# A modulation group moved beside the last two attention heads, and one exponential per block of queries

## The chip, the cores and the metric

The kernel runs on one core of a Trainium2 chip. The metric is device time in microseconds (us) of one execution. The core has five engines: TensorE (PE, matrix products; its weight loads are listed apart as PEld), VectorE (DVE), ScalarE (ACT), GpSimd (POOL) and SyncE (SP), which issues most of the transfers. Each engine works through its own queue in order and waits at an instruction until its data and buffers are there. TensorE writes its results to PSUM, eight banks of 128 partitions x 512 fp32; everything else lies in SBUF.

## The reference

One inference step of a backbone with two layers, width 1024, on 1154 positions: 128 context tokens, a gap of 2, and 1024 latent tokens on a grid 64 wide. In each layer a mixer and a feed-forward part read a normalised input that is scaled and shifted by modulation vectors, and are added back through a gate. The change lies in the modulation and the attention of layer 0:

```python
mc = jnp.split(sc @ w_mod[i] + b_mod[i], N_MOD, axis=-1)    # context: 6 vectors of 1024
ml = jnp.split(sl @ w_mod[i] + b_mod[i], N_MOD, axis=-1)    # latent tokens
hl = rmsnorm(xl, norm_mix[i]) * (1 + ml[1]) + ml[0]         # needed first
q, k, v, p = even_project(hl, w_in_ab[j], q_gain[j], k_gain[j])
# per row of the grid and head; kb, vb: an 8-row neighbourhood; ck, cv: 256 cached context keys
s_loc = jnp.einsum("bqhd,bkhd->bhqk", qi, kb) * scale + bi[None]
s_ctx = jnp.einsum("bqhd,bkhd->bhqk", qi, ck) * scale
pr = jax.nn.softmax(jnp.concatenate([s_loc, s_ctx], axis=-1), axis=-1)
out = pr[..., :n_local] @ vb + pr[..., n_local:] @ cv
...
xl = xl + ml[2] * yl                                        # needed after the out projection
hl = rmsnorm(xl, norm_ffn[i]) * (1 + ml[4]) + ml[3]
xl = xl + ml[5] * conv_ffn(hl, ...)
```

So the six modulation vectors of a layer are six slices of one product of two rows (`sc`, `sl`) with a 1024 x 6144 matrix. The kernel computes them as three *groups* of 2048 columns: group 0 holds vectors 0 and 1, group 1 holds 2 and 3, group 2 holds 4 and 5. Only group 0 is needed before the projections; groups 1 and 2 are first used after the attention. Softmax is taken over 384 local positions (with some masked by the bias) and 256 context keys together.

## The kernel before

**Numbers.** Values are f32. For TensorE each operand is split into a high part and a rest (`whi` and `wlo` of a weight, `hhi` and `hlo` of the input), and a product is three matmuls. A weight block of 128 x 1024 is loaded into `wraw` (L237), copied to `whi` on ScalarE (L253), and the rest `wlo` is made on GpSimd (L255). `wraw`, `whi` and `wlo` have two buffers each in the pool `wp`.

**Order.** Python generators emit the work, and a scheduler then orders the instructions of each engine by data, priorities and buffers.

**A modulation group** (`mod_group`) has 16 *steps*, eight blocks of 128 input channels by two halves of the columns. A step loads 512 KB of `wmod` (L301, tile `mraw`) and issues two f32 matmuls of 512 columns each (L304, `sc` holds the two rows, padded to 32; the profile has four records for a step); their sum stands in the tile `modps`, in one PSUM bank for the group's whole time. The two matmuls of a step and those of its neighbour write different quarters of that bank's partitions (`g = 64 * u + 32 * x`). At the end `mod_spread` turns the result into columns (tiles `modev`, `modt`) with a few small matmuls.

**Layer 0's mixer**, in the order of time:

1. Norm and group 0 (to some 66 us).
2. `project_v`: the values of nine blocks of tokens in two passes, six and three blocks (PSUM `vps`, six banks of the pool `psm`). Each pass reads the four `wv` blocks.
3. `project_qk` for the first pair of heads, in chunks of up to 386 tokens, eight channel blocks with three matmuls each (L650 to L652, PSUM `qps`). ScalarE copies a chunk out and squares it (L656, `qsq`). These chunks and group 1 share the two banks of the pool `psa` (tag `aux`).
4. `project_p` and the pooling (to some 206 us).
5. The attention: eight heads (0 to 7) with five units each, one of context tokens and four of latent tokens. A latent unit has two blocks of 128 queries, called a *pair* in the text: context scores `C` of both blocks in one bank (2 x 256), local scores `S` of each (384). Softmax: maximum of `C` on VectorE (L725); the bias is added to `S` and its maximum taken in one pass that writes into `prob` (L727); on ScalarE an exponential of `C` from PSUM (L738) and one of the local part (L741), each with its total; the totals are added (L745). Then the probabilities are transposed on TensorE (L868, `tp`), copied to `pth` (ScalarE, L872) and split into `ptl` (VectorE, L873), and multiplied with the values (L895, L900, PSUM `O`). Values are read back for each unit (`vr`, L801) and split to `vt`; a head's q and k in split form are `qs` and `ks`.
6. The trunk: out projection (weights `woab`), feed-forward part, and layer 1.

**What fills in.** In each unit the attention calls `filler` twice. In heads 0 to 5 it emits pieces of `project_qk` for later pairs (`RQ` = 3 per call), in heads 6 and 7 it emits `RM` = 1 step of group 2, whose sum uses the single bank of `psg`. Group 2 has its loads go through the buffers of `wraw`, `whi` and `wlo` in turn. Group 1 was emitted earlier: one step at each of the eight channel blocks of the second pass of `project_v` (`EK`, `ER`), and the others between the pieces of `project_qk` for the first pair. Its loads use the two buffers of `prob`, which the attention doesn't need yet.

```python
for what in ORDER:                       # ORDER = "SXfTVg", for each unit
    if what == "S": ... soft = scored(*now)        # scores of this unit
    elif what == "X": prob = soft()                # its softmax
    elif what == "T": pts = turned(last[2][0], ...)# transposes of the unit before
    elif what == "V": valued(...)                  # its product with the values
    elif what in "fg": filler(*now, 0)
```

## Time and profile before

| | |
|---|---|
| median of 3 runs | 2671.11 us (2669.97 to 2671.5) |
| profiled execution, its own time | 2672.02 us |
| span of its profile | 2670.2 us |
| granted TensorE clock, mean over the span | 0.989 |
| TensorE busy (weight loads) | 98% (88%) of the span |
| VectorE, ScalarE, GpSimd busy | 56%, 43%, 49% |

The span is the time from the first to the last instruction of the profiled execution; times in the rows count from its start. The granted clock is a share of full speed: 1.00 is 2.4 GHz, 0.50 is 1.2 GHz, and a mean between says how much of a stretch was spent at each. "Idle before" is the time that an engine stood still ahead of an instruction, and behind "<-" is what ended it.

### The profile page before, as it was taken

To read this page: it belongs to the slowest core of one execution; us is meant where nothing else is said; L and a number is where in the kernel's file an instruction comes from. 1 tells how busy PE (TensorE), PEld (TensorE's weight loads), DVE (VectorE), ACT (ScalarE), POOL (GpSimd) and SP (SyncE) were. 2 spreads that over 40 slices of the span, in tenths; PEclk is the share of its full clock that TensorE was granted. 3 is DMA by queue.
4 is the path that set the end of the run, shared out by engine and by line. 5 is a ranking of instruction groups with operands and counts; after the bars stand their busy time and mean duration, and the time that the engine had idled before them with its cause. 6 is when DMAs were issued, how large, how long until landed. Compare 5 with 4: busy or idle time off the path is not lost.

```text
span 2670.2 us, 38723 instructions
## 1 busy us (share of the span) xinstructions
PE 2604.2 (98%) x14982; PEld 2352.7 (88%) x14982; DVE 1507.0 (56%) x2386; ACT 1139.3 (43%) x1767; POOL 1303.8 (49%) x781
## 2 busy tenths in 40 slices
PE   6999998999999999999999999999999999999999
PEld 4698897799999999989998889899999999888887
DVE  6136777553556556545997844379964344444444
ACT  4315666635432333354555354555324323433332
POOL 2222333156544444334646254689757544555553
PEclk9999998999999999999999999999999999999999
DMA  7622324564465655453335553232222222433332
GB/s 286 206 67 79 72 73 115 164 227 135 153 214 167 207 196 191 152 174 131 130 128 165 184 179 97 86 94 64 80 64 79 79 80 72 127 95 95 94 94 89
DMA packets 139735, 345.89 MB, mean 130 GB/s; under 512 B 46112, under 2 KB 51872, under 8 KB 139552
## 3 DMA queue, kind: packets, MB, share of 16 engines
q1 hardware_dynamic: 139552, 343.41, 40.3%
q8 instruction: 119, 1.95, 0.3%
q14 instruction: 64, 0.52, 0.1%
HBM read 291.97 MB, written 46.67 MB: 127 GB/s over the span
## 4 chain that ended last, share of the span: by engine, by line
PE 90%; DVE 5%; DMA 2%; ACT 1%; POOL 1%; issue 1%; SPq 0%; POOLq 0%; DVEq 0%; ACTq 0%
PE mm L265 17%; PE mm L269 17%; PE mm L267 17%; PE mn L265 8%; PE mn L267 8%; PE mn L269 8%; PE mm L466 2%; PE O L900 2%; PE qps L650 1%; PE qps L651 1%; PE tp L868 1%; PE qps L652 1%; DVE dacc L1008 1%; PE modps L304 1%; PE vps L622 1%
## 5 line engine op out<-in xcount | busy, mean ns | idle before, releaser
L255 POOL TENSOR_TENSOR wlo<-wraw,whi 128x1024 fp32r<-128x1024 f32 x280 | 675.1, 2416 | 797.1 <-ACT whi L253 776.7
L253 ACT ACTIVATE whi<-wraw 128x1024 fp32r<-128x1024 f32 x348 | 364.8, 1057 | 725.5 <-PE mm L267 405.8
L269 PE MATMUL mm<-h,wlo 128*128 128x332 f32 (+6 forms) x2208 | 558.1, 323 | 0.5 <-POOL wlo L255 0.4
L267 PE MATMUL mm<-h,whi 128*128 128x332 f32 (+6 forms) x2208 | 557.5, 323 | 0.0
L265 PE MATMUL mm<-h,whi 128*128 128x332 f32 (+6 forms) x2208 | 555.5, 322 | 0.5 <-DVE ao L911 0.5
L265 PEld LDWEIGHTS mm<-h,whi 128*128 128x128 f32 x2208 | 381.1, 188 | 12.7 <-issue 0.7
L269 PEld LDWEIGHTS mm<-h,wlo 128*128 128x128 f32 x2208 | 379.8, 188 | 12.2 <-POOL wlo L255 1.0
L267 PEld LDWEIGHTS mm<-h,whi 128*128 128x128 f32 x2208 | 378.3, 188 | 11.8 <-issue 1.7
L449 DVE SCALAR_TENSOR_TENSOR x<-mm,mod,x 128x128 f32<-128x128 f32 (+7 forms) x408 | 212.5, 561 | 150.2 <-PE mm L269 141.6
L1008 DVE SCALAR_TENSOR_TENSOR dacc<-u,params,dacc 128x661 f32<-128x661 f32 (+1 forms) x344 | 285.4, 830 | 7.6
L265 PE MATMUL mn<-h,whi 128*128 128x494 f32 (+1 forms) x672 | 262.4, 391 | 2.0 <-DVE x L449 2.0
L267 PE MATMUL mn<-h,whi 128*128 128x494 f32 (+1 forms) x672 | 262.1, 390 | 0.0
L269 PE MATMUL mn<-h,wlo 128*128 128x494 f32 (+1 forms) x672 | 260.5, 390 | 0.0
L1104 DVE SCALAR_TENSOR_TENSOR facc<-mm,params,facc 128x663 f32<-128x663 f32 (+3 forms) x92 | 82.1, 892 | 305.6 <-ACT facc L1103 305.4
L1116 POOL TENSOR_TENSOR facc<-facc,facc 128x664 f32<-128x664 f32 (+3 forms) x88 | 126.8, 1441 | 152.3 <-DVE facc L1106 152.3
L1104 DVE SCALAR_TENSOR_TENSOR facc<-mn,params,facc 128x493 f32<-128x493 f32 (+1 forms) x84 | 62.0, 738 | 217.3 <-ACT facc L1103 217.3
L265 PE MATMUL mm<-fh,whi 128*128 128x332 f32 (+2 forms) x720 | 171.1, 317 | 4.1 <-DVE x L449 2.3
L990 POOL TENSOR_TENSOR acc<-acc,tap 128x508 f32<-128x508 f32 (+1 forms) x104 | 151.5, 1460 | 38.6 <-ACT tap L989 31.8
L267 PE MATMUL mm<-fl,whi 128*128 128x332 f32 (+2 forms) x720 | 169.4, 315 | 0.0
L269 PE MATMUL mm<-fh,wlo 128*128 128x332 f32 (+2 forms) x720 | 168.9, 314 | 0.0
L449 DVE SCALAR_TENSOR_TENSOR x<-mn,mod,x 128x510 f32<-128x510 f32 (+1 forms) x168 | 120.5, 737 | 63.9 <-PE mn L269 63.1
L1119 ACT ACTIVATE fh<-facc 128x664 fp32r<-128x664 f32 (+3 forms) x88 | 60.2, 684 | 217.1 <-POOL facc L1116 217.1
(227 smaller groups left out, 4508.6 us busy)
## 6 DMA issues: line engine op xcount, KB each, us to landing
wraw<-in_fi_dram SPq DMA_DIRECT2D x176, 512.0 KB
wraw<-in_fo_dram SPq DMA_DIRECT2D x88, 512.0 KB
mraw<-in_wmod_dram SPq DMA_DIRECT2D x48, 512.0 KB
mraw<-in_wmod_dram SPq DMA_DIRECT2D x96, 256.0 KB
wraw<-in_pw_dram SPq DMA_DIRECT2D x48, 512.0 KB
lowi<-wlo SPq DMA_DIRECT2D x44, 512.0 KB
wlo<-lowi SPq DMA_DIRECT2D x44, 512.0 KB
lowo<-wlo SPq DMA_DIRECT2D x22, 512.0 KB
```

What stands on the lines that cost most here:

```text
L253: nc.scalar.activation(hi, raw, AF.Copy)
L255: (eng or nc.gpsimd).tensor_tensor(lo, raw, hi.bitcast(F32), op=ALU.subtract)
L265: mm(pv, whi, xhi[:, a:b], start=start, stop=False)
L267: mm(pv, whi, xlo[:, a:b], start=False, stop=False)
L269: mm(pv, wlo, xhi[:, a:b], start=False, stop=stop)
L449: nc.vector.scalar_tensor_tensor(xd[:, a:b], pv, gate[:, d, st:st + 1], xd[:, a:b], op0=ALU.mult, op1=ALU.add)
L466: mm(ps[:, c, :n], w[:, s], x[k][:, o:o + n], start=a, stop=b)
L990: nc.gpsimd.tensor_tensor(acc[:, :n], acc[:, :n], p[:, :n], op=ALU.add)
L1008: nc.vector.scalar_tensor_tensor(acc[:, :n] if t == NCK - 1 else pacc, u[:, t:t + n], wk(i, t), acc[:, :n] if t == side else pacc, op0=ALU ...
L1104: nc.vector.scalar_tensor_tensor(acc[:, 1:W], part.ps(ps, 0, W - 1), w(0), acc[:, 1:W], op0=ALU.mult, op1=ALU.add)
L1116: (nc.gpsimd if side or part.n == 1 else nc.vector).tensor_tensor(a[:, :W], a[:, :W], g[:, :W], op=ALU.mult)
L1119: nc.scalar.activation(hi[:, :W], a[:, :W], AF.Copy)
```

## The change

Two things are changed together.

**Group 1 is emitted elsewhere.** `project_v` and the pieces of `project_qk` for the first pair no longer emit steps of group 1 (`EK`, `ER`, the argument `between` and the loads through `prob` are gone). In heads 6 and 7 `mods` now holds both groups, 1 and then 2, and `filler` emits two steps per call (`RM` = 2). Both take the single bank of `psg`, one after the other, and load through the buffers of `wp`.

**One exponential per block of queries.** VectorE's maximum of `C` for both blocks becomes a pass for each block that adds zero (`self.one[:, 0:1]`, a column of zeros), takes the maximum and writes the scores into `prob` behind the local ones. ScalarE then has one exponential over all 640 columns in SBUF, with one total. The addition of two totals goes.

```diff
-RM = 1
+RM = 2
-EK = 0
-ER = 1
...
-    def mod_group(self, l, m, pool, psp, ev, tag="aux", mtag="wraw", last=None):
+    def mod_group(self, l, m, pool, psp, ev, tag, last):
...
-                if mtag == "prob":
-                    raw = pool.tile([P, 2, 640], F32, tag="prob", name=self.nm("mraw"), bufs=2)
-                    raw = raw.rearrange("p a b -> p (a b)")[:, :1024]
...
+                t = ("wraw", "whi", "wlo")[(2 * k + u) // 2 % 3]
+                raw = pool.tile([P, 1024], F32, tag=t, name=self.nm("mraw"), bufs=2)
...
-                if js[0] and k >= EK:
-                    self.pull(between, ER)
...
-        nc.vector.tensor_reduce(mx[:, 0, :n], C[:, :, :w], op=ALU.max, axis=AX.X)
+        for i in range(n):
+            nc.vector.tensor_tensor_reduce(out=p[:, i, nl:nl + w], in0=C[:, i, :w],
+                                           in1=self.one[:, 0:1].to_broadcast([P, w]), op0=ALU.add, op1=ALU.max,
+                                           scale=1.0, scalar=-3.0e38, accum_out=mx[:, 0, i:i + 1])
...
-            nc.scalar.activation(p[:, i, nl:nl + w], C[:, i, :w], AF.Exp, bias=bi, scale=1.0,
+            nc.scalar.activation(p[:, i, :nl + w], p[:, i, :nl + w], AF.Exp, bias=bi, scale=1.0,
                                  accum_out=sm[:, i, 0:1])
-            if Ls:
-                nc.scalar.activation(p[:, i, :nl], p[:, i, :nl], AF.Exp, bias=bi, scale=1.0,
-                                     accum_out=sm[:, i, 1:2])
-        tot, rc = st[:, 3, 0], st[:, 4, 0]
-        if Ls:
-            nc.vector.tensor_tensor(tot[:, :n], sm[:, :n, 0], sm[:, :n, 1], op=ALU.add)
-            nc.vector.reciprocal(rc[:, :n], tot[:, :n])
-        else:
-            nc.vector.reciprocal(rc[:, :n], sm[:, :n, 0])
+        rc = st[:, 4, 0]
+        nc.vector.reciprocal(rc[:, :n], sm[:, :n, 0])
...
-                early = [self.mod_group(0, 1, ap, self.psa, evac, mtag="prob")]
-                self.project_v(hhi, hlo, ready, wv, up, early)
+                self.project_v(hhi, hlo, ready, wv, up)
...
                 for _ in range(7):
                     next(g0, None)
-                    self.pull(early, 1)
...
-                mods = [self.mod_group(0, 2, self.wp, self.psg, evac, tag="g", last=(self.pst, "w"))]
+                mods = [self.mod_group(0, m, self.wp, self.psg, evac, tag="g", last=(self.pst, "w")) for m in (1, 2)]
```

The next rows show where this moves instructions. A name's number is that of one tile; a row is an instruction of the program with the tiles that it writes and reads.

TensorE before, between the two passes of `project_v` (`vps_320` is of the first pass, `vps_613` of the second):

```order
L625 MATMUL vps_320<-whi_553,hlo_508 128x512 x3
L304 MATMUL modps_614<-mraw_647,sc 32x512 x2
L304 MATMUL modps_614<-mraw_666,sc 32x512 x2
L622 MATMUL vps_613<-whi_621,hhi_303 128x512
L623 MATMUL vps_613<-wlo_622,hhi_303 128x512
L622 MATMUL vps_613<-whi_621,hhi_303 128x512
L623 MATMUL vps_613<-wlo_622,hhi_303 128x512
L622 MATMUL vps_613<-whi_621,hhi_303 128x512
```

TensorE in the changed program, the same place; lines 614 to 617 there are lines 622 to 625 of before:

```order
L617 MATMUL vps_319<-whi_553,hlo_508 128x512 x3
L617 MATMUL vps_320<-whi_553,hlo_508 128x512 x3
L614 MATMUL vps_613<-whi_616,hhi_303 128x512
L615 MATMUL vps_613<-wlo_617,hhi_303 128x512
L614 MATMUL vps_613<-whi_616,hhi_303 128x512
L615 MATMUL vps_613<-wlo_617,hhi_303 128x512
L614 MATMUL vps_613<-whi_616,hhi_303 128x512
L615 MATMUL vps_613<-wlo_617,hhi_303 128x512
```

The two steps of group 1 between the passes are gone, and so are the others behind them.

TensorE before, in head 7, at the last two steps of group 2 (`modps_4492`):

```order
L304 MATMUL modps_4492<-mraw_5025,sc 32x512 x2
L900 MATMUL O_4771<-pth_4760,vt_4628 128x256 x2
L900 MATMUL O_4771<-ptl_4761,vt_4628 128x256 x2
L900 MATMUL O_4771<-pth_4767,vt_4628 128x128 x2
L868 MATMUL tp_4839<-consts,prob_4729 128x128 x4
L304 MATMUL modps_4492<-mraw_5073,sc 32x512 x2
L900 MATMUL O_4771<-ptl_4768,vt_4628 128x128 x2
L868 MATMUL tp_4848<-consts,prob_4729 128x128 x2
L895 MATMUL O_4855<-consts,st_4730 64x128 x2
```

TensorE in the changed program, at the last five steps of group 2 (`modps_4737`); lines 298, 856 and 888 there are L304, L868 and L900 of before:

```order
L888 MATMUL O_4986<-ptl_4976,vt_4868 128x256 x2
L888 MATMUL O_4986<-pth_4982,vt_4868 128x128 x2
L298 MATMUL modps_4737<-mraw_4953,sc 32x512 x2
L888 MATMUL O_4986<-ptl_4983,vt_4868 128x128 x2
L298 MATMUL modps_4737<-mraw_4957,sc 32x512 x2
L298 MATMUL modps_4737<-mraw_5005,sc 32x512 x2
L298 MATMUL modps_4737<-mraw_5009,sc 32x512 x2
L298 MATMUL modps_4737<-mraw_5043,sc 32x512 x2
L349 MATMUL modt_5049<-consts,modev_5047 128x8 x4
L856 MATMUL tp_5056<-consts,prob_4942 128x128 x4
```

Before, matmuls of the attention stand between the last two steps. Now four steps stand one behind another, and the small matmuls of `mod_spread` (`modt`) come right after.

SyncE's queue before, at the last load of group 2 (`mraw_5073`); `cat` is the attention's output and the pooling in memory:

```order
L301 DMA mraw_5073<-in_wmod_dram 128x1024
L1301 DMA cat_5370<-cat_66 128x664
L801 DMA vr_4993<-vd 128x1x64 x4
L237 DMA wraw_5438<-in_woab_dram 128x1024
L237 DMA wraw_5444<-in_woab_dram 128x1024
L801 DMA vr_5077<-vd 128x1x64 x4
L237 DMA wraw_5450<-in_woab_dram 128x1024
L237 DMA wraw_5644<-in_woab_dram 128x1024
L801 DMA vr_5162<-vd 128x1x64 x4
L237 DMA wraw_5705<-in_woab_dram 128x1024
```

SyncE's queue in the changed program, at the last loads of group 2 (`mraw_4957` to `mraw_5043`):

```order
L295 DMA mraw_4957<-in_wmod_dram 128x1024
L789 DMA vr_5100<-vd 128x1x64
L295 DMA mraw_5005<-in_wmod_dram 128x1024
L295 DMA mraw_5009<-in_wmod_dram 128x1024
L295 DMA mraw_5043<-in_wmod_dram 128x1024
L235 DMA wraw_5374<-in_woab_dram 128x1024
L235 DMA wraw_5380<-in_woab_dram 128x1024
L235 DMA wraw_5386<-in_woab_dram 128x1024
L235 DMA wraw_5580<-in_woab_dram 128x1024
L235 DMA wraw_5641<-in_woab_dram 128x1024
```

Before, the first loads of `woab` stand between the loads of values for head 7. Now the loads of group 2 end one behind another, and five loads of `woab` come right behind them.

On every engine the order of the trunk's instructions is the same in both programs.

## Rows read from the trace of the kernel before

**Rows 1.** The page: busy time by engine, chain by engine, GpSimd's costliest group.

```profile
PE 2604.2 (98%) x14982; PEld 2352.7 (88%) x14982; DVE 1507.0 (56%) x2386; ACT 1139.3 (43%) x1767; POOL 1303.8 (49%) x781
...
PE 90%; DVE 5%; DMA 2%; ACT 1%; POOL 1%; issue 1%; SPq 0%; POOLq 0%; DVEq 0%; ACTq 0%
...
L255 POOL TENSOR_TENSOR wlo<-wraw,whi 128x1024 fp32r<-128x1024 f32 x280 | 675.1, 2416 | 797.1 <-ACT whi L253 776.7
```

**Rows 2.** Busy time by stretch: us, engines, granted clock (PEclk), DMA share, GB/s.

```profile
0.00:66.00 66.00, 43.59 (x224) 29.67 (x224) 40.74 (x53) 28.15 (x35) 13.84 (x17) 0.99 0.80 289
66.00:147.00 81.00, 75.71 (x329) 53.72 (x330) 8.25 (x14) 23.49 (x34) 23.47 (x15) 0.91 0.58 192
...
206.00:447.00 241.00, 228.83 (x1555) 212.04 (x1553) 173.89 (x443) 155.55 (x416) 79.63 (x61) 0.95 0.30 79
447.00:522.00 75.00, 65.93 (x410) 47.23 (x409) 52.42 (x144) 50.42 (x137) 21.11 (x16) 0.93 0.51 150
```

**Rows 3.** Groups of instructions on TensorE, 66 to 147 us.

```profile
L304 PE MATMUL modps<-mraw,sc 128*32 128x512 f32 x64 | 15.6, 619 | 2.4 <-DMA mraw<-in_wmod_dram 2.4
```

**Rows 4.** TensorE's timeline: start, us from there, line, idle time before.

```profile
82.88 1.06 PE L304 MATMUL modps<-mraw,sc 128*32 128x512 f32 x8
...
88.97 1.05 PE L304 MATMUL modps<-mraw,sc 128*32 128x512 f32 x4 [0.39 <-DMA mraw<-in_wmod_dram]
...
104.59 1.05 PE L304 MATMUL modps<-mraw,sc 128*32 128x512 f32 x4
105.58 0.50 PE L625 MATMUL vps<-whi,hlo 128*128 128x512 f32 x1
105.91 0.34 PE L650 MATMUL qps<-hhi,whi 128*128 128x386 f32 x1
...
115.93 0.69 PE L650 MATMUL qps<-hhi,whi 128*128 128x384 f32 x1 [2.88 <-ACT qsq L656]
...
128.59 1.07 PE L304 MATMUL modps<-mraw,sc 128*32 128x512 f32 x8
...
134.42 1.05 PE L304 MATMUL modps<-mraw,sc 128*32 128x512 f32 x4 [1.50 <-DMA mraw<-in_wmod_dram]
```

**Rows 5.** Timeline of SyncE's queue, 84 to 92.5 us.

```profile
91.73 0.34 SPq L237 DMA_DIRECT2D wraw<-in_wv_dram  x1
```

**Rows 6.** ScalarE's timeline, 95 to 104 us.

```profile
95.96 1.06 ACT L253 ACTIVATE whi<-wraw 128x1024 fp32r<-128x1024 f32 x1 [6.46 <-DMA wraw<-in_wv_dram]
```

**Rows 7.** Two stretches at the lower clock, columns as in rows 2.

```profile
115.30:122.10 6.80, 6.17 (x19) 6.18 (x20) 0.00 (x0) 2.90 (x4) 0.00 (x0) 0.50 0.76 296
135.80:139.20 3.40, 3.40 (x13) 3.40 (x12) 0.00 (x0) 0.42 (x1) 1.48 (x5) 0.50 0.81 272
```

**Rows 8.** TensorE's timeline, 449 to 475 us.

```profile
449.62 2.78 PE L304 MATMUL modps<-mraw,sc 128*32 128x512 f32 x24 [0.61 <-DVE qk L672]
```

**Rows 9.** TensorE's waits, 447 to 522 us: total, times, longest.

```profile
PE O L900 <- DVE ptl L873: 2.9, 2, 2.0
...
PE C L713 <- DMA ks<-ks: 1.6, 1, 1.6
```

**Rows 10.** Groups on ScalarE by shape, 206 to 522 us.

```profile
L741 ACT ACTIVATE prob<-prob,st 128x384 f32<-128x384 f32 x64 | 38.9, 608 | 0.0
...
L738 ACT ACTIVATE prob<-C,st 128x256 f32<-128x256 f32 x64 | 30.1, 470 | 23.4 <-DVE st L733 22.9
L738 ACT ACTIVATION_READ_ACCUMULATOR prob<-C,st 128x1 f32 x72 | 14.2, 197 | 0.0
```

**Rows 11.** Groups on VectorE by shape, 206 to 522 us.

```profile
L727 DVE CUSTOM_DVE_ANT_1 prob<-S,trr 128x384 f32<-128x384 f32 x64 | 33.4, 552 | 13.5 <-PE tp L868 7.6 <-PE S L714 5.9
...
L725 DVE TENSOR_REDUCE st<-C 128x2 f32<-128x512 f32 x32 | 21.9, 685 | 14.3 <-PE C L714 14.1
...
L727 DVE DVE_READ_ACCUMULATOR2_ANT st<- 128x1 f32 x64 | 5.3, 82 | 0.0
```

**Rows 12.** TensorE's waits, 206 to 447 us, columns as in rows 9.

```profile
PE O L900 <- DVE ptl L873: 4.2, 5, 2.2
```

More of the change, by code (lines that the diff above doesn't have):

```diff
@@ L294, in mod_group @@
             for u in range(2):
-                if mtag == "prob":
-                    raw = pool.tile([P, 2, 640], F32, tag="prob", name=self.nm("mraw"), bufs=2)
-                    raw = raw.rearrange("p a b -> p (a b)")[:, :1024]
-                else:
-                    t = mtag if mtag == "mraw" else ("wraw", "whi", "wlo")[(2 * k + u) // 2 % 3]
-                    raw = pool.tile([P, 1024], F32, tag=t, name=self.nm("mraw"), bufs=1 if t == "mraw" else 2)
+                t = ("wraw", "whi", "wlo")[(2 * k + u) // 2 % 3]
+                raw = pool.tile([P, 1024], F32, tag=t, name=self.nm("mraw"), bufs=2)
                 nc.sync.dma_start(raw, self.i["wmod"][l, m, k, :, u * 1024:(u + 1) * 1024])
@@ L306, in mod_group @@
                 yield
-        self.mod_spread(l, m, ps, ev, *(last or (psp, tag)))
+        self.mod_spread(l, m, ps, ev, *last)
         yield
@@ L605, in project_p, with project_v @@
         return finish
-    def project_v(self, hhi, hlo, ready, wv, sp, between):
+    def project_v(self, hhi, hlo, ready, wv, sp):
         nc = self.nc
@@ L737, in softmax @@
             bi = neg[:, i:i + 1]
-            nc.scalar.activation(p[:, i, nl:nl + w], C[:, i, :w], AF.Exp, bias=bi, scale=1.0,
+            nc.scalar.activation(p[:, i, :nl + w], p[:, i, :nl + w], AF.Exp, bias=bi, scale=1.0,
                                  accum_out=sm[:, i, 0:1])
-            if Ls:
-                nc.scalar.activation(p[:, i, :nl], p[:, i, :nl], AF.Exp, bias=bi, scale=1.0,
-                                     accum_out=sm[:, i, 1:2])
-        tot, rc = st[:, 3, 0], st[:, 4, 0]
-        if Ls:
-            nc.vector.tensor_tensor(tot[:, :n], sm[:, :n, 0], sm[:, :n, 1], op=ALU.add)
-            nc.vector.reciprocal(rc[:, :n], tot[:, :n])
-        else:
-            nc.vector.reciprocal(rc[:, :n], sm[:, :n, 0])
+        rc = st[:, 4, 0]
+        nc.vector.reciprocal(rc[:, :n], sm[:, :n, 0])
         if late:
@@ L1223, in mixer0 @@
                     next(g0, None)
-                    self.pull(early, 1)
                 fin = None
```

## Prediction

> **What bounds the kernel now.** I read the page first. TensorE is busy for 98% of the span, and the chain that ended last stands on it for 90% [rows 1]. So a change pays by what it takes out of TensorE's queue, by the waits between two of its instructions, or by the time that TensorE spends at the lower of its two clocks (1.2 of 2.4 GHz). The stretches come next [rows 2]: before 66 us TensorE is held by the first transfers (289 GB/s, 22 us idle), and what the change touches lies behind that, in three places. From 66 to 147 us (values, first q and k, modulation group 1) TensorE is idle for 81 - 75.7 = 5.3 us, and its mean clock is 0.91. From 206 to 447 us (heads 0 to 5) it is idle for 12.2 us at 0.95, and from 447 to 522 us (heads 6 and 7, group 2) for 9.1 us at 0.93. A mean clock of 0.95 over 241 us is 24 us at 1.2 GHz, which costs 12 us; 0.93 over 75 us is 10.5 us, which costs 5.2. TensorE's timeline, its waits and the timelines of the engines that feed it then say what stands in each gap.
>
> **Group 1 leaves the first place.** Its 16 steps hold TensorE for 15.6 us, and for another 2.4 us TensorE waits for their loads [rows 3]. They also hold one of the two banks that q and k are projected into: the wait of 2.9 us that ends at 115.93 us is for that, since the second chunk needs a bank whose copy ScalarE has not made yet [rows 4]. With two banks, two chunks run before one is missed, and I count this wait as gone. (The few small matmuls that spread a group's result move along, and cancel.)
>
> Not all of it is saved, because the steps also covered other waits:
> - The pair of steps at 82.88 us runs while ScalarE empties the banks for the next three token blocks. That wait takes its place: 1.0 us back.
> - In the pass over these blocks (82.88 to 105.91 us, 23.0 us) the pair, four lone steps of 0.99 us and a wait of 0.4 lie between 17.7 us of matmuls, 4.4 us for each of four weight blocks [rows 4]. The last block's load is issued at 91.73 us, its whi runs from 95.96 us for 1.06, and its wlo on GpSimd takes 2.4, so it is ready at 99.5 us [rows 1, 5, 6]. Without the two steps ahead of the pass (0.99 us and, at half the clock, twice that) the first block starts 3.0 us earlier, at 80.9 us, and this one is wanted at 80.9 + 3 x 4.4 = 94.1 us. If its chain moves by the same 3.0 us, it is ready at 96.5: a wait of 2.4 us. With no modulation loads ahead of it the transfer should take less than its 4.2 us, so I take 2.0, between nothing and all four steps (4.0).
> - The pair at 128.59 us covers a weight conversion. Tiny matmuls stand there now; I give back 0.5 us.
>
> The clock: it was at 1.2 GHz from 115.3 to 122.1 us, where the 2.9 us wait ends, and from 135.8 to 139.2 us, right after a wait of 1.5 us for a load [rows 4, 7]. Both waits go, which would give back (6.8 + 3.4) / 2 = 5.1 us. The wait for a weight block may bring a stretch of its own, so I count half, 2.5.
>
> Sum: 15.6 + 2.4 + 2.9 - 1.0 - 2.0 - 0.5 + 2.5 = **19.9 us saved**. Upper bound (no wait for weights, none at 128 us, all of the clock): 25.0. Lower bound (the 2.9 us stay, all four lone steps turn into waits, no clock): 12.5.
>
> **Group 1 arrives in heads 6 and 7.** A lone step takes 0.99 us (104.59 to 105.58), but six in a row take 2.78 us [rows 4, 8], so two neighbours cost what one costs: they write different quarters of the bank's partitions. Before, group 2 was six in a row and ten alone: 2.8 + 9.9 = 12.7 us. The order of the change has, for group 1, six in a row, a pair and eight alone (11.7 us), and for group 2 nine alone, three in a row and four in a row (13 turns of 0.99, 12.9 us): 24.6 us. Added: **11.9 us**. Two steps per turn do not make pairs, since the scheduler puts matmuls of the attention between most of them.
> The Trainium skill ("TensorE: Matmul & The Clock Gate", Part 3, row/col tiling) says that matmuls in different column tiles run at the same time, and gives a measured 2.38x for three. If that held across what stands between two steps, 32 steps would be 16 pairs of 1 us, 8.6 less than my count, and the sum below would be 24 instead of 15. The trace bears it out for neighbours only: the lone step of 0.99 us has matmuls of other tiles on both sides.
>
> What of the 11.9 us is hidden? TensorE idles for 9.1 us here, 2.9 of it before O for the split of the transposed probabilities and 1.6 for `ks` [rows 2, 9]. The steps lie before the last 30 rows of PE's order, so only part of the idle time is near one: I take 3 us as filled. Another 2 us I take off for the lighter softmax (below). Against that, two loads of group 1 now stand in SP's queue ahead of head 6's `ks`: 1 MB at the 289 GB/s of rows 2 is 3.6 us; between nothing and that, I take 1. So **+7.9 us**, between -2.4 (all idle time filled and the clock up) and +20.0 (nothing filled, `ks` in full, and 4.5 us of waits for loads: the 2.4 us of rows 3 came with 14 loads, here are 26).
> The five loads of the next weights (`woab`) move behind the last load of group 2. I cost that at nothing: behind the use of that load stand 30 rows of PE, the transposes and products of three units, over 10 us of work, against 4.2 + 1.06 + 2.4 us for a load and its conversion [rows 1, 5, 6]. ScalarE's queue has the first whi ahead of a copy that TensorE needs, so if the cover is short, about 4 us (the load) are lost.
>
> **The softmax.** On ScalarE a block had exponentials of 470 and 608 ns, each with an accumulator read of 197 [rows 10]: 1472 ns. Now it has one over 640 columns, between 608 and 1078 ns; I take 840, so 1037 with its read: 435 ns less, 28 us over 64 blocks (between 13 and 43). On VectorE a pair of blocks had one maximum pass of 685 ns [rows 11]. Now it has two passes over 256 columns, which also write them to SBUF. Each lies between 343 (half of 685) and 552 ns (the pass over 384 columns); I take 420 and a read of 82, so 1004 ns, 10 us more over 32 pairs (a small sum of two totals goes, which I don't count). Neither engine sets the pace: both are under three quarters busy in rows 2. What counts is that the bank of the context scores is free after VectorE's passes and not after ScalarE's third exponential, and that a pair's probabilities come some 0.55 us earlier (0.87 less on ScalarE, 0.32 more on VectorE). In heads 0 to 5 TensorE waited 4.2 us for the split of the transposed probabilities [rows 12]. I take **-3 us** there, between -10 (these 4.2 and half of the lost clock) and +7.6 (below).
>
> **Sum.** -19.9 + 7.9 - 3 = -15.0 us. The profiled execution took 2672.0 us (span 2670.2 and 1.8 around it); the runs' median is 0.9 lower. So 2657.0 in such an execution, and 2656 us as a median.
>
> **Rivals.** A measurement of this kernel can tell about 0.2%, 5.3 us, from no change.
> - *It fills better* (2646 us, chance 0.18): the clock comes back fully in the first place and no weight is waited for (25.0), and 5 us more are filled in heads 6 and 7: -25. For it: 34 us at the lower clock lie in the heads. Against it: the attention's own chains stay as long as they are in most respects.
> - *The weights take over* (2663, 0.14): the first place gains its lower bound of 12.5, in all -7.6. For it: ScalarE already stood idle for 6.5 us before the `wv` load [rows 6]. Against it: 8 MB less go through the queues there, at 192 GB/s so far.
> - *VectorE holds back* (2667, 0.08): the maxima are known 0.32 us later, and in heads 0 to 5 all 24 pairs pass that on: +7.6 instead of -3, in all -4.4. Against it: the later part of the same chain is shorter.
> - *The loads come late*, the other side (2677, slower, 0.10): in heads 6 and 7 SP issues 26 loads of 512 KB between `vr` loads that wait for their buffers. If each were waited for like the three in the first place (2.4 / 3 = 0.8 us), that is 20.8 us, in all +5.8; from 0.58 us per load on the gain is gone. Against it: of the loads in the same place none shows among the longest waits [rows 9], and the transfers there move 150 GB/s. The Trainium skill ("DMA: Bandwidth & Descriptors", Latency and other measured facts) gives an HBM access 0.2 us on average and 2 us under high load, which would lengthen each load just there; no row separates that part.
>
> My forecast has a chance of 0.50. Below 2665.8 us lie it, the first rival and most of the second: faster 0.78. Same 0.14, slower 0.08. The bounds of the terms reach from 2634 to 2686; 8 in 10 of the chance lies from **2643 to 2669**.
>
> **What the profile will show.** No matmul of a modulation group between 66 and 440 us; the work that ended at 206 us ends 16 to 23 us earlier; a new wait of TensorE for wlo near 95 us; at most one stretch at 1.2 GHz between 90 and 150 us; exponentials of 640 columns near 0.84 us; heads 6 and 7 some 8 us longer; the rest as before. I am wrong if TensorE waits for modulation loads in the heads, if the weight wait is over 4 us, or if heads 0 to 5 take longer than 241 us.

## The result, and the profile after

The changed kernel takes 2651.75 us (median of 4 runs, 2648.94 to 2656.77), 0.993 of the kernel before (95% interval 0.9913 to 0.9948). Two further sets of runs, with runs of before beside them, gave 0.9946 (0.9934 to 0.9958) and 0.9946 (0.9933 to 0.9958), 2655.4 and 2653.68 us. (The kernels of one such comparison run in turn, in the same rounds.) So it is faster by 14 to 19 us. The forecast was 2656, with 2643 to 2669 as the range.

The page of the changed kernel, its busy time and its chain, which answer to [rows 1]:

```profile
PE 2585.2 (98%) x14982; PEld 2341.3 (88%) x14982; DVE 1502.9 (57%) x2458; ACT 1125.6 (43%) x1639; POOL 1304.9 (49%) x781
...
PE 91%; DVE 4%; ACT 2%; DMA 1%; POOL 1%; issue 1%; SPq 0%; POOLq 0%; DVEq 0%; ACTq 0%
```

TensorE is as busy as before in shares; the span is 23.3 us shorter (2646.9 against 2670.2). To see where, I cut both spans at three marks that exist in both: the first `O` of head 0, the first modulation step in head 6, and the first matmul of the out projection (`mm<-h`). The stretches between them, by the view of busy time by stretch (columns as in rows 2), of the changed kernel:

```profile
212.21:416.64 204.43, 193.32 (x1414) 179.93 (x1414) 151.53 (x460) 130.10 (x299) 74.70 (x55) 0.98 0.30 76
416.64:498.95 82.31, 77.52 (x468) 48.59 (x469) 52.01 (x160) 43.60 (x95) 20.10 (x13) 0.96 0.75 230
498.95:2646.90 2147.95, 2130.90 (x12092) 1953.81 (x12091) 1204.02 (x1695) 867.13 (x1122) 1151.07 (x659) 1.00 0.40 130
```

And the same two stretches of the kernel before:

```profile
242.05:449.62 207.57, 198.96 (x1412) 182.98 (x1412) 154.93 (x408) 139.28 (x389) 72.36 (x54) 0.97 0.29 74
449.62:522.01 72.39, 64.16 (x397) 45.94 (x397) 50.53 (x139) 47.85 (x130) 20.38 (x15) 0.93 0.52 153
```

Until the first `O` the changed kernel takes 212.21 us instead of 242.05 (-29.8), for heads 0 to 5 204.43 instead of 207.57 (-3.1), for heads 6 and 7 82.31 instead of 72.39 (+9.9), and for the trunk 0.2 less. The sum is -23.3. The forecast had -19.9, -3, +7.9 and 0.

TensorE's timeline of the changed kernel has the waits that took the place of those in [rows 4] and [rows 9]:

```profile
66.69 0.50 PE L614 MATMUL vps<-whi,hhi 128*128 128x512 f32 x1 [0.34 <-ACT hhi L534]
...
75.83 0.50 PE L614 MATMUL vps<-whi,hhi 128*128 128x512 f32 x1 [0.96 <-ACT vst L620]
...
80.70 0.50 PE L615 MATMUL vps<-wlo,hhi 128*128 128x512 f32 x1 [0.20 <-POOL wlo L253]
...
94.66 0.44 PE L642 MATMUL qps<-hhi,whi 128*128 128x386 f32 x1 [1.37 <-ACT whi L251]
...
97.10 0.44 PE L644 MATMUL qps<-hhi,wlo 128*128 128x386 f32 x1 [1.47 <-POOL wlo L253]
...
416.64 2.78 PE L298 MATMUL modps<-mraw,sc 128*32 128x512 f32 x24 [1.04 <-DVE qk L664]
...
422.03 1.05 PE L298 MATMUL modps<-mraw,sc 128*32 128x512 f32 x4
...
425.04 1.05 PE L298 MATMUL modps<-mraw,sc 128*32 128x512 f32 x4 [1.96 <-DMA mraw<-in_wmod_dram]
```

The pair of steps that covered ScalarE's copies is replaced by a wait of 0.96 us (forecast 1.0). The weight blocks of this second pass cost 0.20 us, and the first block of q 1.37 for `whi` and 1.47 for `wlo`. In head 6 the first six steps stand in a row as before, and one load is waited for, 1.96 us; it parts the two steps at 422.03 and 425.04 us that the forecast counted as a pair.

One number runs through all that follows: the time that TensorE spent at 1.2 GHz. I take it from the granted clock in windows of 1 us between 20 and 530 us (a window at 0.75 counts half). It was 51.2 us in the profile of before and 20.5 in that of the changed kernel, and costs half of itself. 15.3 of the 23.3 us between these two executions are that.

### The profile page after: what moved, and what is told of

Its sections match the earlier page's. It is cut to its first block, busy times and chain, and to the rows that moved or that the text cites. A ratio compares the mean times of both kernels' runs of the same rounds, so it can differ in the third digit from the quotient of the medians.

```text
span 2646.9 us, 38655 instructions
## 1 busy us (share of the span) xinstructions
PE 2585.2 (98%) x14982; PEld 2341.3 (88%) x14982; DVE 1502.9 (57%) x2458; ACT 1125.6 (43%) x1639; POOL 1304.9 (49%) x781
## 4 chain that ended last, share of the span: by engine, by line
PE 91%; DVE 4%; ACT 2%; DMA 1%; POOL 1%; issue 1%; SPq 0%; POOLq 0%; DVEq 0%; ACTq 0%
PE mm L263 17%; PE mm L267 17%; PE mm L265 17%; PE mn L263 8%; PE mn L265 8%; PE mn L267 8%; PE mm L460 2%; PE O L888 1%; PE qps L642 1%; PE qps L644 1%; PE qps L643 1%; PE tp L856 1%; DVE dacc L996 1%; PE modps L298 1%; PE qrb L662 1%
## 5 line engine op out<-in xcount | busy, mean ns | idle before, releaser
L267 PEld LDWEIGHTS mm<-h,wlo 128*128 128x128 f32 x2208 | 379.8, 188 | 12.2 <-POOL wlo L253 1.0
```

The lines of the kernel that those rows point to most:

```text
L267: mm(pv, wlo, xhi[:, a:b], start=False, stop=stop)
```

## The experiments

All profiles in one table, in us. Each row is one profiled execution; "at 1.2 GHz" is the sum just defined.

| kernel | until first O | heads 0 to 5 | heads 6, 7 | trunk | at 1.2 GHz | ratio of runs (95%) |
|---|---|---|---|---|---|---|
| before | 242.1 | 207.6 | 72.4 | 2148.2 | 51.2 | 1 |
| changed | 212.2 | 204.4 | 82.3 | 2148.0 | 20.5 | 0.993 (0.9913 to 0.9948) |
| changed, second | 214.7 | 204.8 | 83.3 | 2150.8 | 30.7 | 0.9946 (0.9934 to 0.9958) |
| changed, third | 213.7 | 204.7 | 83.0 | 2149.1 | 20.5 | 0.9946 (0.9933 to 0.9958) |
| softmax alone | 239.7 | 202.6 | 71.1 | 2149.4 | 34.1 | 0.9981 (0.9973 to 0.999) |
| move alone | 212.7 | 204.6 | 84.9 | 2149.0 | 23.9 | 0.9946 (0.9934 to 0.9958) |
| group 1 short | 215.8 | 204.7 | 75.8 | 2150.0 | 34.1 | 0.9918 (0.9906 to 0.9931) |
| two early loads | 220.5 | 204.0 | 83.4 | 2151.2 | 27.3 | 0.9962 (0.995 to 0.9975) |
| bank held, first try | 217.8 | 204.8 | 83.5 | 2148.1 | 34.1 | 0.993 (0.9917 to 0.9944) |
| bank held | 220.4 | 204.7 | 83.6 | 2150.9 | 34.0 | 0.9974 (0.9964 to 0.9984) |
| conversions on GpSimd | 214.1 | 201.6 | 83.0 | 2149.0 | 20.4 | 0.9933 (0.992 to 0.9945) |
| four quarters | 217.0 | 204.7 | 77.6 | 2148.1 | 34.1 | 0.9919 (0.9905 to 0.9932) |
| four quarters + conversions | 211.5 | 201.1 | 82.0 | 2148.8 | 27.2 | 0.9928 (0.9914 to 0.9941) |
| before with four quarters | 233.0 | 203.7 | 69.4 | 2149.4 | 37.5 | 0.9961 (0.9949 to 0.9973) |

**The changed kernel again**, unchanged, twice.

> The changed kernel once more, for a second profile and a closer ratio. Two accounts of the 23.3 us between the two profiled executions. A: some 20 us of it are steady (16 steps and their waits out of the first place, a 3.2 us wait for hlo that went with them, less the 10 us that heads 6 and 7 grew), and the rest is TensorE time at 1.2 GHz, which was 51.2 us before and 20.5 us after and differs from execution to execution. Then the median is near 2652 us, the runs spread over some 6 to 8 us, and the time until the first O of head 0 in a second profile is 25 to 30 us below the 242.05 us of before. B: the clock is as steady as the rest; then this profile shows 20 us at 1.2 GHz again and a time within 2 us of 2649.

> The changed kernel as it is, on the chip of the three others, for a comparison in the same rounds: 2651 to 2656 us, 0.993 to 0.995 of before, and a profile with 20 to 35 us at 1.2 GHz.

The medians are 2655.4 and 2653.68 us, and the runs of the changed kernel reach from 2648.9 to 2656.9. The three profiles agree within 2.5 us in the first stretch, 0.4 in heads 0 to 5 and 1.0 in heads 6 and 7. The time at 1.2 GHz was 20.5, 30.7 and 20.5. The first account holds, with the median 3 us above what it named: a part of the clock's gain is there in one execution and not in the next. Against the two profiles whose order until head 0 is that of before (242.1 and 239.7, mean 240.9) the three (mean 213.5) are 27.4 us earlier.

**The softmax alone**: the kernel before, with the new `softmax`.

> The kernel before with the new softmax alone. My sum: nothing changes until head 0, the heads gain about 3 us, so 2668 us (between 2661 and 2679 by the bounds). Rival: the softmax gave a good part of the gain, since the heads had 24 us at 1.2 GHz before and half of that after; then 2660 us or less, and most of these stretches are gone from the profile.

It takes 2664.81 us against 2668.95, 4.1 less between the medians and 5 us by the ratio (2.7 to 7.2), between the 3 of my sum and the 9 of the rival.

**The move alone**: the changed kernel with the old `softmax`.

> The changed kernel with the old softmax: group 1 moved, and nothing else. My sum, with the first profile after: the first place gains 25 to 30 us and heads 6 and 7 lose 10 to 12, so 2654 to 2659 us, slower than the changed kernel by 2 to 4. Rival (the softmax gave a good part): 2660 us or more. Rival (the two parts hinder each other): as fast as the changed kernel, 2652 us.

It takes 2653.91 us, the same ratio as the whole change in the same rounds. So next to the move the softmax brought nothing that these runs can tell, though by itself it brought some 5 us. 3.4 us of its 5.0 in heads 0 to 5 can be the clock: that stretch had 13.6 us at 1.2 GHz in the profile of before and 6.8 in this one. Whether the two parts really hinder each other, or the scatter of a few us hides it, stays open; a wait that the new softmax brings with it is shown below, with the conversions on GpSimd.

**Group 1 cut short**, to 2 of its 16 steps:

```diff
+        n = KT if m == 2 else 1
-        for k in range(KT):
+        for k in range(n):
```

> The changed kernel, with group 1 summed over the first of its eight blocks of input channels alone (2 of 16 steps; the gates and shifts of group 1 come out other than the reference's). If the steps in heads 6 and 7 cost what they hold TensorE for, 14 fewer save their turns less what fills in, 8 to 10 us: 2642 to 2644 us. If most of them only fill time in which TensorE would wait for the attention, 3 us or less: 2649 us or more. If waits for their loads are part of the cost, the 2.0 us wait at the third step stays or goes with them, and the saving is above 10 us.

2647.27 us, 8 below the changed kernel in the same rounds, at the low end of the 8 to 10 that the first account named; heads 6 and 7 take 75.8 us instead of 82.9 (mean of three). The steps are paid for, but not in full even here: without them a new wait appears in TensorE's timeline of this kernel, the `ks` of head 6, which they had covered:

```profile
429.89 0.44 PE L706 MATMUL C<-ks,qs 128*128 128x128 f32 x1 [5.71 <-DMA ks<-ks]
```

**Two early loads.** Of group 1's first place only the first two loads are put back, into the buffers of `prob`, where nothing reads them:

```diff
+                if js[0] and k < 2:
+                    raw = ap.tile([P, 2, 640], F32, tag="prob", name=self.nm("mraw"), bufs=2)
+                    raw = raw.rearrange("p a b -> p (a b)")[:, :1024]
+                    nc.sync.dma_start(raw, self.i["wmod"][0, 1, k // 2, :, k % 2 * 1024:k % 2 * 1024 + 1024])
```

> The changed kernel with the first two loads of group 1 put back to where they were before, and nothing that uses them (a second load of the same data is made in head 6). Account A (these two loads delay the cached keys, so that VectorE's casts of them stand between two pieces of hlo): TensorE's wait of 3.2 us for hlo near 60 us is back, with 3 to 7 us at 1.2 GHz behind it, and the first O of head 0 comes 5 to 7 us later than in the changed kernel; 2657 to 2661 us. Account B (the wait belongs to the steps on TensorE): no such wait, and the time of the changed kernel.

2660.9 us, 0.9962, where the first try of the next experiment, which never kept its bank, gave 2652.26 in the same rounds: 8.6 us of the gain are gone there, and 4 to 9 by the ratios of the table. TensorE's timeline of the kernel before:

```profile
62.68 1.42 PE L625 MATMUL vps<-whi,hlo 128*128 128x512 f32 x5 [3.23 <-DVE hlo L541]
```

and of this kernel:

```profile
63.31 1.22 PE L621 MATMUL vps<-whi,hlo 128*128 128x512 f32 x2 [3.10 <-DVE hlo L535]
```

The wait for `hlo` is back, though TensorE has no step of group 1 there. VectorE's timeline of this kernel says why:

```profile
58.44 0.83 DVE L535 SCALAR_TENSOR_TENSOR hlo<-x,md,hhi 128x130 fp32r<-128x130 f32 x1
59.30 2.65 DVE L777 CAST ck<-craw 64x256 fp32r<-64x256 f32 x2
61.98 1.55 DVE L535 SCALAR_TENSOR_TENSOR hlo<-x,md,hhi 128x1024 fp32r<-128x1024 f32 x2
```

The casts of cached keys (`ck`) stand between two pieces of `hlo` that TensorE needs. The kernel before has the same rows 0.64 us earlier. VectorE's timeline of the changed kernel has both casts ahead of that whole chain:

```profile
50.16 2.39 DVE L773 CAST ck<-craw 64x256 fp32r<-64x256 f32 x2 [3.21 <-DMA craw<-in_ck_dram]
```

There the keys' loads are no longer behind group 1's in SyncE's queue, and the wait is 0.34 us for `hhi`. The first `O` comes 7.0 us later than the mean of the changed kernel. 2.8 us of that are the longer wait. 10.2 us at 1.2 GHz follow behind it, but this profile has fewer of them later: until the first `O` it has 13.7 us, where the three of the changed kernel have 9.1 in the mean, so 2.3 us are the clock. Some 2 us have no account.

**A bank held.** A tile that nothing needs takes one of the two `aux` banks from the second pass of the values on.

```diff
+            if js[0]:
+                self.held = self.psa.tile([P, 512], F32, tag="aux", name=self.nm("held"))
+                nc.vector.memset(self.held[:, :1], 0.0)
...
+                nc.vector.tensor_tensor(evac()[:, :1], self.held[:, :1], qk[0][-1][:, :1], op=ALU.add)
```

> The changed kernel with one of the two aux banks held from the second pass of the values to the end of the first q and k, by a tile that nothing needs, as group 1's sum held it before. Account A (the 2.9 us wait for qsq is the bank): TensorE waits 2 to 3 us after the first chunk of q, and less behind other chunks; 3 to 6 us longer with the clock. Account B (that wait came from ScalarE's late start on conversions): nothing, within 1 us of the changed kernel up to head 0.

That first try had a plain copy of the tile as its reader, which the scheduler put early, so the bank was free again and the run does not bear on the question: no wait for `qsq`, 2652.26 us. With the reader above, which needs the finished k, the bank stays taken:

> The changed kernel with one aux bank held once more. In the run before this one the tile was read long before the end of the first k, so that its bank came free; now its reader also reads the finished k. Account A (the 2.9 us wait for qsq is the missing bank): a wait of 2 to 3 us behind the first chunk of q or k, shorter ones where ScalarE is free, and the first O of head 0 comes 3 to 7 us later than in the changed kernel. Account B (ScalarE's work at that moment is the cause): no wait above 1 us behind a chunk, and at most 2 us later.

2661.68 us against 2653.68 in the same rounds, and the first `O` 6.9 us later than the mean of the changed kernel. TensorE's waits of this kernel from 90 to 140 us (total, times, longest):

```profile
PE qps L645 <- ACT whi L251: 2.1, 1, 2.1
PE qps L645 <- ACT qsq L651: 1.9, 2, 1.0
PE qps L647 <- POOL wlo L253: 1.8, 1, 1.8
PE mm L460 <- ACT whi L251: 1.0, 1, 1.0
```

So the bank is worth having, by 8 us in the runs. But it shows in two waits of 1 us for `qsq`, a wait of 1.0 us for `whi` of the next product and another 3.4 us at 1.2 GHz (117 to 122 us), not in one wait of 2.9; a part of the 6.9 us is the scatter of the clock, since the first try, with as much time at 1.2 GHz until the first `O`, was 4.2 us late with both banks. The wait of [rows 4] was the bank and ScalarE being late together; the split between them stays open.

**The conversions on GpSimd.** In heads 0 to 5 the wait for `ptl` that I expected to shrink has grown. TensorE's waits of the changed kernel in that stretch:

```profile
PE O L888 <- DVE ptl L861: 8.3, 5, 5.1
```

One of the five lasts 5.1 us and ends at 406.95 us. ScalarE's timeline of the changed kernel before it:

```profile
399.05 0.76 ACT L1288 ACTIVATE h<-cat 128x664 fp32r<-128x664 f32 x1 [4.13 <-DMA cat<-cat]
399.72 0.81 ACT L733 ACTIVATE prob<-prob,st 128x640 f32<-128x640 f32 x1
```

ScalarE stands 4.13 us at the first conversion of the out projection's input, whose load is late, and the two exponentials that VectorE, and through it TensorE, wait for stand behind it.

```diff
-                    nc.scalar.activation(hi[:, :part.w], c[:, :part.w], AF.Copy)
+                    if part is OA and k in order[:4]:
+                        nc.gpsimd.tensor_copy(hi[:, :part.w], c[:, :part.w])
+                    else:
+                        nc.scalar.activation(hi[:, :part.w], c[:, :part.w], AF.Copy)
```

> The changed kernel with the high parts of the first four blocks of the out projection's input made on GpSimd instead of ScalarE. In the changed kernel TensorE waits 5.07 us for ptl at the end of head 5; ScalarE stood 4.1 us before at the first of these conversions, waiting for its load, with two exponentials behind it in its queue. Account A (that queue is the cause): the wait falls to 2 us or less with the 6.8 us at 1.2 GHz behind it partly gone, 3 to 7 us faster than the changed kernel. Account B (VectorE's longer softmax is the cause): the wait stays near 5 us. Account C: GpSimd now stands at the loads in ScalarE's place, values (vt) come late, and the wait moves to O.

TensorE's timeline of this kernel, the wait in that place and the one that came instead:

```profile
403.62 0.50 PE L888 MATMUL O<-pth,cv 128*128 128x256 f32 x2 [0.91 <-DVE ptl L861]
...
425.27 0.79 PE L888 MATMUL O<-ptl,vt 128*128 128x256 f32 x2 [3.10 <-DVE ptl L861]
```

The wait falls to 0.91 us and heads 0 to 5 take 201.6 us, 3 less. So the queue is the cause, not VectorE's longer softmax passes. But it is the new softmax with which the conversion comes to stand there. ScalarE's timeline of the move alone, which has the old one, has the first conversion behind the exponentials, and without a wait:

```profile
399.79 0.60 ACT L733 ACTIVATE prob<-prob,st 128x384 f32<-128x384 f32 x1
...
400.39 0.74 ACT L1292 ACTIVATE h<-cat 128x664 fp32r<-128x664 f32 x1
```

TensorE's longest wait for `ptl` in heads 0 to 5 is 2.2 us there. In the softmax alone ScalarE stands 4.33 us at the conversion with the exponentials behind it, and the longest wait is 3.7.

The kernel's time (0.9933) is that of the changed kernel all the same, and a wait of 3.10 us for `ptl` appears in head 6. VectorE's timeline of this kernel has a piece of `qs` ahead of that `ptl`:

```profile
420.75 2.62 DVE L695 TENSOR_TENSOR qs<-qk,qs 64x128 fp32r<-64x128 f32 x1
```

and GpSimd's the piece of `km` beside it:

```profile
419.71 3.50 POOL L689 TENSOR_TENSOR km<-qk,ks 64x1154 fp32r<-64x1154 f32 x1
```

The last section shows such a piece of `qs` that took 0.28 us with GpSimd idle. It is as long in the changed kernel (2.60 us, at 421.84), where TensorE stands in head 6 for the load of a step instead.

**Four quarters.** The cost of a lone step by itself: a step's 1024 columns as four matmuls of 256 in four quarters of the partitions, instead of two of 512 in two (the spreading of the result follows this layout, and the first of a group's steps alone starts the sum).

```diff
-                for x in range(2):
-                    g = 64 * u + 32 * x
-                    nc.tensor.matmul(ps[g:g + 32, :], self.sc[:, k, :], raw[:, x * 512:(x + 1) * 512],
-                                     start=k == 0, stop=k == KT - 1)
+                for x in range(4):
+                    nc.tensor.matmul(ps[32 * x:32 * x + 32, 256 * u:256 * u + 256], self.sc[:, k, :],
+                                     raw[:, x * 256:(x + 1) * 256], start=k + u == 0, stop=k + u == KT)
```

> The changed kernel with each step of groups 1 and 2 as four matmuls of 256 columns in four quarters of the bank's partitions, instead of two of 512 in two quarters; the spreading of the result follows. Account A (a lone step is dear since it fills two quarters only): a lone step falls from 0.99 us to 0.5 to 0.6, heads 6 and 7 shorten by 21 lone turns of 0.4 to 0.5, less what turns into waits for loads, 6 to 9 us; 2644 to 2648 us. Account B (matmuls of a step run one behind another, or the turn's fixed part decides): a step stays at 0.9 us or more and the time within 2 us of the changed kernel. Account C (the loads set the pace there, at 230 GB/s): steps get short and TensorE waits for mraw in their place; gain under 3 us.

TensorE's timeline of this kernel around two lone steps:

```profile
469.60 0.64 PE L297 MATMUL modps<-mraw,sc 128*32 128x256 f32 x8
470.17 0.66 PE L871 MATMUL tp<-consts,prob 128*128 128x128 f32 x4
470.76 0.64 PE L297 MATMUL modps<-mraw,sc 128*32 128x256 f32 x8
471.33 0.33 PE L903 MATMUL O<-pth,vctx 128*128 128x128 f32 x1
```

The group of all its steps (busy us, mean ns of one | idle before):

```profile
L297 PE MATMUL modps<-mraw,sc 128*32 128x256 f32 x256 | 19.6, 388 | 4.1 <-DMA mraw<-in_wmod_dram 3.2 <-DVE qk L679 0.9
```

A lone step now takes 0.57 us (469.60 to 470.17) instead of 0.99, with the same columns and the same loads. The Trainium skill ("TensorE: Matmul & The Clock Gate", Part 3, row/col tiling) says that matmuls in different column tiles run at the same time; 0.99 / 0.57 = 1.7 for four quarters instead of two is in line with it. Heads 6 and 7 take 77.6 us instead of 82.9, 5.3 less where 6 to 9 were expected, and the steps 19.6 us of TensorE instead of 26.6, while the waits for their loads rise from 2.0 us at most to 3.2. The runs give 2649.61 us, 0.9919, above the 2644 to 2648 expected and 2.7 us below the first try of the held bank in the same rounds.

**Four quarters with the conversions on GpSimd.**

> Both of the edits that removed something: steps of four matmuls in four quarters, and the first four blocks of the out projection's input split on GpSimd. If their gains add, heads 0 to 5 take 201 to 203 us and heads 6 and 7 77 to 79, 5 to 8 us below the changed kernel, 2644 to 2648 us. If the wait of 3.1 us for ptl in head 6, which the second edit brought, stays, 2648 to 2651 us.

2648.16 us, 5.5 below the changed kernel in the same rounds: the second of the two cases. Heads 0 to 5 have the gain (201.1), heads 6 and 7 do not (82.0): the 20.4 us at 1.2 GHz that this profile has behind head 0 lie in them, and the wait in head 6 is still there (2.2 us). This and the one before are the fastest versions that compute everything, 3 to 6 us below the changed kernel's order in their rounds; their intervals overlap that of the first runs of the changed kernel.

**Before, with four quarters.** Is it the place of group 1, or only the dear turns?

> The kernel before, with steps of four matmuls in four quarters: group 1 stays beside the values and the first q and k, with the old softmax. If the steps' turns are most of what group 1 costs there, some 11 lone turns save 0.4 each in the first place and ten in heads 6 and 7: 6 to 9 us, 2661 to 2665 us, still 8 or more above the changed kernel, since the waits for hlo (3.2 us), for the bank and for loads stay. If it comes within 4 us of the changed kernel, the move is not what matters but the turns.

2658.35 us, 10 below before and 4.7 above the changed kernel of the same rounds, between the two cases that were named. Between the medians, cheap turns alone give about two thirds of what the whole change gives. The wait for `hlo` is still there (3.62 us), as it must be if it hangs on the loads. In this profile heads 0 to 5 took 203.7 us, 3.9 less than in the profile of before, though the edit touches nothing there: single profiles of that stretch differ by as much.

## Why the prediction was right, and where it was off

**The first place: mis-sized.** Forecast -19.9, with 25.0 as the upper bound; measured -29.8 in the first pair of profiles and -27.4 between means. The steps, their load waits and the wait for the bank went, as said. The price of covers was close: 0.96 us for ScalarE's copies (1.0), and 0.2 + 1.4 + 1.5 = 3.1 us for weights (2.0), at the first block of q and not at the last block of the values. What failed is the sentence that "what the change touches lies behind" 66 us. Two loads of group 1 stood ahead of the cached keys' loads, that decided the order on VectorE, and the 3.2 us wait at 62.68 us hung on that, with the 6.8 us at 1.2 GHz behind it. Busy time and granted clock of before there, columns as in rows 2:

```profile
64.20:71.00 6.80, 6.80 (x19) 4.45 (x18) 5.04 (x9) 3.00 (x4) 0.00 (x0) 0.50 0.17 64
```

The experiment with two early loads puts this at 7.0 us; 19.9 + 7.0 = 26.9 is near the measured 27.4, but some 2 of the 7.0 have no account.

**The clock: too cautious for the first profile.** I counted 2.5 us of it in the first place. There the time at 1.2 GHz fell from 27.2 us to 6.8 (13.6 and 6.8 in the other two profiles), which is worth 7 to 10 us, 3.4 of them behind the `hlo` wait. From 60 us to head 0 the profile of before has three waits above 2 us (3.2, 2.9, 2.3), each with a stretch at 1.2 GHz at its end or behind it. I priced one of them, together with the wait of 1.5 us, at half. The clock behind the `hlo` wait is also part of the 7.0 us above and is not to be added to them: between the means the clock is worth 7.4 us (23.9 us at 1.2 GHz against 9.1), and without the stretches behind `hlo` (8.5 in the mean) 3.1, near the 2.5 that I counted.

**Heads 6 and 7: right, a little low.** Forecast +7.9, measured +9.9 to +10.9. TensorE's group of steps, before and in the changed kernel:

```profile
L304 PE MATMUL modps<-mraw,sc 128*32 128x512 f32 x64 | 13.3, 601 | 0.6 <-DVE qk L672 0.6
```

```profile
L298 PE MATMUL modps<-mraw,sc 128*32 128x512 f32 x128 | 26.6, 602 | 3.0 <-DMA mraw<-in_wmod_dram 2.0 <-DVE qk L664 1.0
```

TensorE's time in them rose by 13.3 us, where I counted 11.9 by turns; 1.0 of the difference is the pair of group 1 that a load wait parted. TensorE's idle time fell by 3.4 us (8.2 to 4.8; by 1.6 to 1.9 in the other two profiles), where I took 3 as filled. The lighter softmax is 2.0 us between the move alone (84.9, one profile) and the mean of the changed kernel, as taken, with a scatter of 1.0. `ks` was not late by more than 0.4; loads of steps were, by 1.4 to 2.0 in all. I had named such a wait as a sign of being wrong: it came, at a tenth of its rival's price.

**The softmax: prices right, the -3 us luck.** ScalarE's group of the changed kernel from the first `O` on, which answers to [rows 10]:

```profile
L733 ACT ACTIVATE prob<-prob,st 128x640 f32<-128x640 f32 x62 | 50.9, 822 | 31.0 <-DVE st L728 30.8
```

VectorE's, which answer to [rows 11]:

```profile
L718 DVE CUSTOM_DVE_ANT_0 prob<-C,one 128x256 f32<-128x256 f32 x62 | 24.2, 419 | 22.6 <-PE C L706 13.4 <-PE tp L856 9.1
...
L718 DVE DVE_READ_ACCUMULATOR2_ANT st<- 128x1 f32 x69 | 5.7, 82 | 0.0
```

822 ns for the long exponential (840 taken) and 419 for the maximum with its copy (420). Heads 0 to 5 came out at -3 as forecast, but not because the wait for `ptl` shrank: it grew from 4.2 us to 8.3, by the queue on ScalarE shown above. Nor is the -3 shown to be the softmax: with the old one the stretch took 204.6 us in the move alone and 203.7 in the kernel before with four quarters, as short as with the new one (202.6 to 204.8 where the conversions stay on ScalarE). The time is made up otherwise. TensorE idles there for 6.3 to 8.6 us in the three profiles with the old softmax and for 9.0 to 11.1 in these nine with the new one, and it spends 13.6 us at 1.2 GHz with the old and 6.8 to 10.3 with the new, which is worth 2 to 3 us. The stretch from 206 us that I read as heads 0 to 5 also begins 36 us before the first `O`: 4.4 of its 12.2 us of idle time and 10.2 of its 24 us at 1.2 GHz lie at the pooling, so my bound of -10 was too wide.

**The cover of the `woab` loads** held: the trunk begins without a wait and takes 2148.0 us against 2148.2.

**The rivals.** Loads that come late cost 2.0 us in the heads, not 20.8. VectorE's longer passes did not hold TensorE back. The weights took 3.1 us (3.4 and 3.8 in the other two profiles), not the 7.4 by which their rival cut the gain. The first rival's 2646 us were nearly reached by one execution of 2648.9, by the `hlo` wait and the clock in the first place and not by better filling in the heads. Of the signs, the work that ended at 206 us came 28 us earlier and not 16 to 23, and the first step in head 6 stands at 416.64 us, ahead of the 440 that I named, as it had to by my own sum. Against the profile of before, the mean of the three profiles is 28.5 us shorter in the first place (8.6 more than forecast), 2.9 in heads 0 to 5, 10.5 longer in heads 6 and 7 (2.6 more) and 1.1 longer in the trunk (scatter: the same instructions took 2148.0 to 2151.2 there). So the errors cancel in part, which is luck too, and the sum of 2657.0 for such an execution was 4 to 6 us too high.

## What to carry to other kernels

A load that is moved takes its place in the queue with it: look up which small loads stood behind it, and which engine's order hung on them, far ahead of where the moved work itself ran. An engine that gets less to do may get another order: here the shorter softmax on ScalarE came with a conversion ahead of the exponentials, at a load that was late. Price a wait of 2 us on a busy TensorE at its length and what the lower clock behind it costs where it comes, and read single profiles with that in mind. And a narrow product that stands alone was cheaper here with its columns spread over all four quarters (0.57 us instead of 0.99): that needs no scheduler to find it a neighbour.

## What the runs showed of the hardware

The clock is not settled by the program. The eleven profiles without group 1 in the first place have the same pair of waits at the first block of q (near 95 us, with two early loads near 102), 0.9 to 2.3 us each. In four of them TensorE stayed at 2.4 GHz, in seven it fell to 1.2 for 3.4 or 6.8 us. The same stretch of the changed kernel in its first profile:

```profile
96.00:98.00 2.00, 0.90 (x5) 0.91 (x6) 0.00 (x0) 1.98 (x3) 1.96 (x2) 1.00 1.03 409
98.00:100.00 2.00, 2.00 (x13) 2.00 (x12) 0.00 (x0) 1.98 (x3) 1.47 (x1) 1.00 1.05 280
```

and in its second:

```profile
96.00:98.00 2.00, 1.13 (x4) 0.67 (x3) 0.00 (x0) 1.61 (x3) 1.96 (x2) 0.50 0.98 374
98.00:100.00 2.00, 2.00 (x8) 2.00 (x7) 0.00 (x0) 1.98 (x3) 1.70 (x1) 0.50 0.89 243
```

Over all 15 runs of the changed kernel, the five below 2652.3 us had a mean granted clock of 0.995 or 0.996 and the eight from 2654.0 up one of 0.992 to 0.994; 0.003 of 2650 us is 8 us, as far as its runs lie apart. The executions of the first two profiles differ by 6.7 us, of which 5.1 are the clock, 3.4 of these in this stretch.

VectorE waits for GpSimd. VectorE's timeline of the kernel before has two casts of 64x256 that took 0.59 us together, with GpSimd idle until 46.22 us:

```profile
45.73 0.59 DVE L785 CAST ck<-craw 64x256 fp32r<-64x256 f32 x2 [0.53 <-DMA craw<-in_ck_dram]
```

and a single one that took 2.34 us:

```profile
58.66 2.34 DVE L785 CAST ck<-craw 64x256 fp32r<-64x256 f32 x1
```

GpSimd's timeline of the same kernel has its `wlo` beside that one:

```profile
58.44 2.42 POOL L255 TENSOR_TENSOR wlo<-wraw,whi 128x1024 fp32r<-128x1024 f32 x1
```

The cast ends at 61.00 us, 0.14 behind `wlo` (60.86). The Trainium skill ("SBUF — State Buffer", SBUF: two separate sides) says that the two engines share a pair of ports that is locked for a whole instruction; these rows agree. Which mode the cast ran in, no row shows. It is a part of the `hlo` wait: of the 2.65 us of both casts there, some 2 us are this.

The pieces of `qs` show it more often. VectorE's timeline of the changed kernel has two of one shape:

```profile
196.69 0.28 DVE L695 TENSOR_TENSOR qs<-qk,qs 64x128 fp32r<-64x128 f32 x1
...
201.83 2.73 DVE L695 TENSOR_TENSOR qs<-qk,qs 64x128 fp32r<-64x128 f32 x1 [0.27 <-ACT qs L692]
```

GpSimd's timeline of the same kernel has it idle at the first and busy at the second:

```profile
201.75 2.66 POOL L689 TENSOR_TENSOR km<-qk,ks 64x1154 fp32r<-64x1154 f32 x1 [10.88 <-ACT ks L686]
```

The second piece ends 0.15 us behind `km`. The other six of this shape took 1.17 to 3.40 us; each has a `km` beside it and ends 0.14 to 0.16 us behind an instruction of GpSimd.
